# Bias tables of an encoder kernel: 32 copies of each bias row made by the matmul, a 128-partition store, and a skewed read back in four pieces

## The chip, the cores and the metric

The kernel runs on one core of one Trainium2 chip. The metric is the device time of one execution in microseconds (us). Before the change three runs took 1973.15, 1976.38 and 1978.78 us; the median is 1976.38 us.

## What is computed

The reference is a two-layer encoder over a sample of 512 tokens and a prompt of 256 tokens, width 1024. Layer 0 mixes tokens with a gated linear recurrence (4 heads of 128, 64-token chunks, both directions) and with dilated band attention: three groups of four heads of 64, with windows and dilations (128, 1), (512, 4) and (2048, 16). Layer 1 mixes with a gated 31-tap depthwise convolution. Each layer ends with a squared-ReLU MLP of width 4096 and layer norms.

The change touches one piece of the attention, its additive bias:

```python
rel = c - QB - a                                   # key position minus query position
valid = (np.abs(rel) <= half)[None] & (key_idx >= 0) & (key_idx < L)
bias = jnp.transpose(bias_table[t5_buckets(rel * r)], (2, 0, 1))
s = jnp.einsum('brhnqd,brhnkd->brhnqk', qb, kb) * (dh ** -0.5) + bias[:, None]
s = jnp.where(valid, s, NEG_INF)
```

The bias of a head depends on the relative position alone: 383 values per head (`RELW`), looked up in a table of 32 buckets by 12 heads, plus the band limit (a very large negative number outside it).

## The kernel before, in words

Tokens of both inputs stand side by side (768 columns: 512 sample, 256 prompt). Every large product is made of three products of a high and a low half (`split`, lines 132 to 135: ScalarE copies a tile to the high half, `wh` or `x0h`, VectorE or GpSimd subtracts to get the low half, `wl` or `x0l`). Weights come in units of 128x1024 floats: `advance` (lines 137 to 147) loads one through SyncE's queue into one of 3 `raw` buffers and splits it. `gemm_fm` (line 167) turns one unit into 128 output features for all tokens: 24 matmuls of 512 columns and 24 of 256, in two of the three PSUM buffers with the tag `g`. `gemm_tm` (line 181) makes token-major products.

Layer 0 (`ab_layer`) goes: load and split the input (`load_x`), make the bias tables (`bias_tables`), then for each attention group `attn_gemm` (four units of queries and keys, drained by ScalarE at line 454 and VectorE at line 456, then six token tiles of values, drained at lines 471 and 473) and `attention` (jobs of score, softmax, transpose and value product, six jobs in group 0 and three in each of the others). Groups 1 and 2 write their values to DRAM (`dv<-mv`, line 479) and read them back permuted (line 485). Then follow `cross_group`, the recurrence, and the rest.

`bias_tables` needs, for each group, a tile in which partition p holds, for each of the four heads, the bias row shifted by p. It multiplies the bucket table by a one-hot matrix (line 408, 4 partitions out), adds the band limit on VectorE into a row tile (line 412, or a copy at line 414), stores the row 128 times to DRAM from these 4 partitions with GpSimd's queue (line 416, `bt<-qq`), and reads it back with a stride of 382 floats per partition, which makes the skew (line 421, `r<-bt`). For groups 1 and 2 VectorE adds block masks to it (lines 426 and 428). The row tile has the tag `qq`, and there is one buffer of it: the next group's row waits until the store of this one has landed. At the end a selection matrix is loaded into the one `e` buffer and copied by GpSimd to `selr` (lines 431 to 433), which takes the same `qq` buffer. The `e` and `at` buffers are also those in which every second attention job keeps its scores (line 522); the `mv` buffers (two) hold one-hot rows, block masks and later the values of groups 1 and 2.

The order of the instructions on each engine is fixed when the kernel is built, by a scheduler with its own model of what each instruction costs; each engine then works through its own queue in that order and waits where an operand or a buffer is not ready. GpSimd's DMA issues stand in GpSimd's queue, and a DMA that must wait for another holds what is behind it there.

Of the kernel before, what the change touches and what calls it, by code (L numbers as in the profile page):

```python
# [11 lines left out]
F32 = mybir.dt.float32  # L12
# [3 lines left out]
ALU = mybir.AluOpType  # L16
# [4 lines left out]
P = 128  # L21
# [4 lines left out]
T = TS + TP  # L26
# [36 lines left out]
NEG = -1e30  # L63
# [3 lines left out]
BUCKETS = 32  # L67
MAXDIST = 1024
TAPS = 31
HALO = TAPS // 2  # L70
RELW = 383
UPAD = TS + TP + 3 * HALO
UOUT = TS + TP + HALO
SEG = ((0, TS), (TS, TP))
AB = {"g": 8, "e": 1, "at": 1, "qq": 1, "mv": 2, "oa": 4, "ob": 6}
# [3 lines left out]
def _buckets(rel):  # L79
    half = BUCKETS // 2  # L80
    exact = half // 2
    n = np.abs(rel)
    large = exact + (np.log(np.maximum(n, 1) / exact) / np.log(MAXDIST / exact) * (half - exact)).astype(np.int32)
    large = np.minimum(large, half - 1)
    return np.where(rel > 0, half, 0) + np.where(n < exact, n, large)


def _fm(w):
    n = w.shape[1] // P
    return w.reshape(KD, P, n, P).transpose(2, 1, 0, 3).reshape(n, P, D)  # L90


def _bm(w, nf):
    k = w.shape[0] // P
    q = D // nf
    n = w.shape[1] // nf
    return w.reshape(k // q, q, P, n, nf).transpose(0, 3, 2, 1, 4).reshape(k // q, n, P, D)


class Kernel:  # L100
# [292 lines left out]

    def bias_tables(self):
        nc, i = self.nc, self.i
        rb = self.sb(self.abc, [BUCKETS, 12], "rb")
        nc.gpsimd.dma_start(rb, i["rel_bias"])
        oh = self.t("e")[0:BUCKETS].rearrange("p (a b) -> p a b", a=2)
        oh2 = self.t("mv")[0:BUCKETS, 0:384]
        nc.gpsimd.dma_start(oh[:, :, 0:RELW], i["onehot"][:, 0:2, :])  # L400
        nc.gpsimd.dma_start(oh2[:, 0:RELW], i["onehot"][:, 2, :])
        bm = self.t("at")[0:4].rearrange("p (a b) -> p a b", a=2)
        nc.gpsimd.dma_start(bm[:, :, 0:RELW], i["band"].partition_broadcast(4))
        self.bt = []
        for g in range(3):
            p = self.ps("s")
            src = oh[:, g, 0:RELW] if g < 2 else oh2[:, 0:RELW]
            mm = nc.tensor.matmul(p[0:4, 0:RELW], rb[:, 4 * g : 4 * g + 4], src, start=True, stop=True)
            self.after(mm, self.mark, SYNC)
            row = self.sb(self.ap, [P, 2, T], "qq", bufs=AB["qq"])[0:4, 0, 0:384]  # L410
            if g < 2:
                nc.vector.tensor_tensor(row[:, 0:RELW], p[0:4, 0:RELW], bm[:, g, 0:RELW], ALU.add)
            else:
                nc.vector.tensor_copy(row[:, 0:RELW], p[0:4, 0:RELW])
            dt = self.dram.tile([4, P, RELW], F32, tag=f"bt{g}", name=f"bt{g}")
            nc.gpsimd.dma_start(dt, row[:, None, 0:RELW].to_broadcast([4, P, RELW]))
            t = self.sb(self.rp, [P, D], "r")
            w = 256 if g == 0 else 128
            shift = RELW // 2 - (64 if g == 0 else 0)
            src = bass.AP(tensor=dt.tensor, offset=dt.offset + shift, ap=[[RELW - 1, P], [P * RELW, 4], [1, w]])  # L420
            nc.gpsimd.dma_start(t[:, 0 : 4 * w].rearrange("p (h c) -> p h c", h=4), src)
            if g:
                bk = self.t("mv")[:, 0 : 2 * P].rearrange("p (a b) -> p a b", a=2)
                nc.gpsimd.dma_start(bk, i["block"][:, 2 * (g - 1) : 2 * g, :])
                v = t.rearrange("p (s h c) -> p s h c", s=2, h=4)
                nc.vector.tensor_tensor(v[:, 1], v[:, 0], bk[:, 1][:, None, :].to_broadcast([P, 4, P]), ALU.add)
                if g == 2:
                    nc.vector.tensor_tensor(v[:, 0], v[:, 0], bk[:, 0][:, None, :].to_broadcast([P, 4, P]), ALU.add)
            self.bt.append(t)
        sel = self.t("e")[0:12]  # L430
        nc.gpsimd.dma_start(sel, i["sel"].rearrange("r j p -> r (j p)"))
        self.selr = self.sb(self.ap, [P, 2, T], "qq", F32R, AB["qq"])[0:12, 0, :].rearrange("r (j p) -> r j p", j=6)
        nc.gpsimd.tensor_copy(self.selr.rearrange("r j p -> r (j p)"), sel)
# [681 lines left out]
def layout(x_prompt, x_sample, rel_bias, hgrn_lb, w_in_ab, hgrn_norm, w_out_ab, w_in_c, b_in_c, dw_c, dw_b_c, cnorm_g,  # L1115
           cnorm_b, w_out_c, b_out_c, ln_mix_g, ln_mix_b, mlp_w1, mlp_w2, ln_ffn_g, ln_ffn_b):
    a = {k: np.asarray(v, dtype=np.float32) for k, v in locals().items()}
    x = np.concatenate([a["x_sample"][0], a["x_prompt"][0]], 0)
    w = a["w_in_ab"][0]
    hw = 5 * AW  # L1120
    bcols = []
    for g in range(3):
        for part in range(2):
            s = hw + part * BW + g * 256
            bcols.append(w[:, s : s + 256])
    acols = []
    for h in range(4):
        for part in (0, 2, 3, 4):
            s = part * AW + h * P
            acols.append(w[:, s : s + P])  # L1130
    woab = a["w_out_ab"][0]
    woab = np.concatenate([woab[AW:], woab[:AW]], 0)
    rel = np.arange(RELW) - RELW // 2
    onehot = np.zeros((BUCKETS, 3, RELW), np.float32)
    band = np.zeros((2, RELW), np.float32)
    for g, (win, r) in enumerate(GROUPS):
        b = _buckets(rel * r)
        onehot[b, g, np.arange(RELW)] = 1.0
        if g < 2:
            band[g] = np.where(np.abs(rel) <= win // (2 * r), 0.0, NEG)  # L1140
    idx = np.arange(P)
    block = np.zeros((P, 4, P), np.float32)
    for n, ln in enumerate((128, 64, 32, 16)):
        block[:, n, :] = np.where(idx[:, None] // ln == idx[None, :] // ln, 0.0, NEG)
    lmask = np.zeros((P, 5, P), np.float32)
    for n, s in enumerate((1, 2, 4, 8)):
        lmask[:, n, :] = (idx[:, None] // (2 * s) == idx[None, :] // (2 * s)) & (idx[:, None] // s != idx[None, :] // s)
    lmask[:, 4, :] = idx[:, None] // 16 != idx[None, :] // 16
    sel = np.zeros((12, 6, P), np.float32)
    for j in range(6):  # L1150
        sel[2 * j, j, 0:64] = 1.0
        sel[2 * j + 1, j, 64:128] = 1.0
    vec = np.concatenate([
        a["dw_c"][0].T, a["b_in_c"][0].reshape(2, D).T, a["dw_b_c"][0][:, None], a["cnorm_g"][0][:, None],
        a["cnorm_b"][0][:, None], np.zeros((D, 1), np.float32)], 1)
    out = {
        "x": x,
        "xT": x.T.reshape(KD, P, T),
        "w_b": _fm(np.concatenate(bcols, 1)),
        "w_vb": _bm(w[:, hw + 2 * BW :], 256),  # L1160
        "w_va": _bm(w[:, AW : 2 * AW], 512),
        "w_a": _fm(np.concatenate(acols, 1)),
        "w_oab": _bm(woab, 512),
        "w1": np.stack([_fm(a["mlp_w1"][l]) for l in range(DEPTH)]),
        "w2": np.stack([_bm(a["mlp_w2"][l], 512) for l in range(DEPTH)]),
        "w_c": _fm(a["w_in_c"][0]),
        "w_oc": _bm(a["w_out_c"][0], 512),
        "rel_bias": a["rel_bias"],
        "lbT": a["hgrn_lb"].reshape(2, 3, 4, P).transpose(3, 0, 1, 2),
        "gnT": a["hgrn_norm"][0].reshape(4, P).T,  # L1170
        "vecC": vec.reshape(KD, P, 37).transpose(1, 0, 2),
        "bo": a["b_out_c"][0],
        "ln0": np.stack([a["ln_mix_g"][0], a["ln_mix_b"][0]]),
        "ln1": np.stack([a["ln_ffn_g"][0], a["ln_ffn_b"][0]]),
        "ln2": np.stack([a["ln_mix_g"][1], a["ln_mix_b"][1]]),
        "ln3": np.stack([a["ln_ffn_g"][1], a["ln_ffn_b"][1]]),
        "ident": np.eye(P, dtype=np.float32),
        "onehot": onehot,
        "band": band,
        "block": block,  # L1180
        "lmask": lmask,
        "sel": sel,
    }
    return {k: np.ascontiguousarray(v) for k, v in out.items()}
# [13 lines left out]
```

## Time and profile before

| | |
|---|---|
| median of three runs | 1976.38 us (1973.15 to 1978.78) |
| span of the profiled execution, first to last instruction | 1977.0 us |
| PE busy (TensorE matmul) | 1855.2 us, 94% |
| VectorE busy | 1149.4 us, 58% |
| ScalarE busy | 737.5 us, 37% |
| GpSimd busy | 595.4 us, 30% |
| PE busy from 0 to 300 us | 231.79 us |
| PE busy from 300 us to the end | 1623.44 us of 1677 us |

The page gives the span of the profiled execution and no other time of it; the span lies within the spread of the three runs. Busy time of an engine says how long its instructions ran, not what they waited for; the granted clock of TensorE is given as a share of full speed (1.00 is 2.4 GHz, 0.50 is 1.2 GHz).

### The profile page before, as it was taken

To read this page: it belongs to the slowest core of one execution; us is meant where nothing else is said; L and a number is where in the kernel's file an instruction comes from. 1 tells how busy PE (TensorE), PEld (TensorE's weight loads), DVE (VectorE), ACT (ScalarE), POOL (GpSimd) and SP (SyncE) were. 2 spreads that over 40 slices of the span, in tenths; PEclk is the share of its full clock that TensorE was granted. 3 is DMA by queue.
4 is the path that set the end of the run, shared out by engine and by line. 5 is a ranking of instruction groups with operands and counts; after the bars stand their busy time and mean duration, and the time that the engine had idled before them with its cause. 6 is when DMAs were issued, how large, how long until landed. Compare 5 with 4: busy or idle time off the path is not lost.

```text
span 1977.0 us, 26150 instructions
## 1 busy us (share of the span) xinstructions
PE 1855.2 (94%) x10516; PEld 1578.5 (80%) x10516; DVE 1149.4 (58%) x1816; ACT 737.5 (37%) x1200; POOL 595.4 (30%) x355
## 2 busy tenths in 40 slices
PE   5964999999999999999999999889999999999998
PEld 4854787888878888888878989768888789888886
DVE  3221643666676634333469999888995554433336
ACT  3210631233421433333354435644433545423322
POOL 1000100544431000000047668646544468000002
PEclk9986998999999999999999999989999999999999
DMA  5323122111021423333235445433433356412211
GB/s 169 93 49 76 28 78 81 44 44 43 33 97 36 139 96 98 105 96 96 86 102 160 134 141 178 134 110 117 131 96 96 95 160 190 141 54 64 75 43 64
DMA packets 58108, 191.36 MB, mean 97 GB/s; under 512 B 8396, under 2 KB 11532, under 8 KB 57988
## 3 DMA queue, kind: packets, MB, share of 16 engines
q1 hardware_dynamic: 52196, 177.23, 28.9%
q0 software_dynamic: 4928, 9.32, 2.4%
q10 hardware_dynamic: 864, 3.15, 0.5%
q8 instruction: 82, 1.34, 0.3%
q14 instruction: 38, 0.31, 0.1%
HBM read 182.50 MB, written 7.15 MB: 96 GB/s over the span
## 4 chain that ended last, share of the span: by engine, by line
PE 80%; DVE 10%; DMA 4%; issue 3%; ACT 2%; POOL 1%; SPq 0%; DVEq 0%; ACTq 0%; POOLq 0%
PE g L167 41%; PE s L181 24%; PE g L181 7%; PE s L976 3%; DMA raw<-w_b 2%; DMA dv<-mv 2%; DVE qq L731 1%; DVE at L774 1%; DVE x0l L135 1%; ACT wh L134 1%; DVE g L732 1%; DVE w L1078 1%; DVE r L241 1%; PE s L580 1%; PE s L527 0%
## 5 line engine op out<-in xcount | busy, mean ns | idle before, releaser
L134 ACT ACTIVATE wh<-raw 128x1024 fp32r<-128x1024 f32 x320 | 339.0, 1060 | 753.5 <-PE g L167 306.6
L135 POOL TENSOR_TENSOR wl<-raw,wh 128x1024 fp32r<-128x1024 f32 x168 | 411.2, 2457 | 224.2 <-ACT wh L134 223.2
L181 PE MATMUL s<-wh,t 128*128 128x512 f32 x1280 | 398.0, 389 | 1.5 <-DVE r L241 1.5
L167 PE MATMUL g<-x0h,wh 128*128 128x512 f32 x864 | 341.0, 395 | 31.7 <-DVE mv L471 22.3
L135 DVE TENSOR_TENSOR wl<-raw,wh 128x1024 fp32r<-128x1024 f32 x152 | 186.8, 1229 | 268.5 <-ACT wh L134 268.4
L167 PE MATMUL g<-x0l,wh 128*128 128x512 f32 x864 | 339.9, 394 | 0.0
L167 PE MATMUL g<-x0h,wl 128*128 128x512 f32 x864 | 338.7, 392 | 0.0
L181 PEld LDWEIGHTS s<-wh,t 128*128 128x128 f32 x1280 | 240.3, 188 | 52.3 <-DVE r L241 1.9
L167 PE MATMUL g<-x1h,wh 128*128 128x256 f32 x864 | 247.5, 287 | 15.6 <-ACT g L454 15.5
L1017 DVE SCALAR_TENSOR_TENSOR c<-t,vec,c 128x509 f32<-128x509 f32 (+26 forms) x464 | 250.0, 604 | 1.1
L167 PE MATMUL g<-x1h,wl 128*128 128x256 f32 x864 | 247.9, 287 | 1.7 <-DVE wl L135 1.7
L181 PE MATMUL s<-wl,t 128*128 128x512 f32 x640 | 249.1, 389 | 0.0
L167 PE MATMUL g<-x1l,wh 128*128 128x256 f32 x864 | 247.9, 287 | 0.3 <-DVE x1l L135 0.2
L220 POOL TENSOR_TENSOR r<-r,lb 128x512 f32<-128x512 f32 x20 | 29.2, 1482 | 623.2 <-DVE r L219 623.2
L167 PEld LDWEIGHTS g<-x0h,wh 128*128 128x128 f32 x864 | 163.2, 189 | 66.7 <-DVE mv L471 22.5
L241 DVE TENSOR_TENSOR r<-r,s 128x512 f32<-128x512 f32 x164 | 112.1, 684 | 153.9 <-PE s L181 151.3
L167 PEld LDWEIGHTS g<-x0h,wl 128*128 128x128 f32 x864 | 163.3, 189 | 34.5 <-DVE wl L135 0.8
L167 PEld LDWEIGHTS g<-x0l,wh 128*128 128x128 f32 x864 | 163.4, 189 | 33.8 <-DVE x0l L135 1.4
L167 PEld LDWEIGHTS g<-x1h,wh 128*128 128x128 f32 x864 | 167.9, 195 | 18.9 <-ACT g L454 16.0
L939 DVE TENSOR_TENSOR t<-t,t 128x512 fp32r<-128x512 f32 (+1 forms) x112 | 94.4, 843 | 137.2 <-ACT t L938 137.0
L167 PEld LDWEIGHTS g<-x1l,wh 128*128 128x128 f32 x864 | 168.4, 195 | 3.1 <-DVE x1l L135 0.7
L167 PEld LDWEIGHTS g<-x1h,wl 128*128 128x128 f32 x864 | 168.4, 195 | 2.2 <-DVE wl L135 2.0
(335 smaller groups left out, 2525.3 us busy)
## 6 DMA issues: line engine op xcount, KB each, us to landing
raw<-w SPq DMA_DIRECT2D x224, 512.0 KB
raw<-w_c SPq DMA_DIRECT2D x32, 512.0 KB
raw<-w_a SPq DMA_DIRECT2D x16, 512.0 KB
raw<-w_oc SPq DMA_DIRECT2D x16, 512.0 KB
raw<-w_b SPq DMA_DIRECT2D x12, 512.0 KB
raw<-w_oab SPq DMA_DIRECT2D x10, 512.0 KB
raw<-w_vb SPq DMA_DIRECT2D x6, 512.0 KB
r<-x ACTq DMA_DIRECT2D x6, 512.0 KB
```

The lines of the kernel that those rows point to most:

```text
L134: nc.scalar.activation(hi, src, AF.Copy)
L135: return (eng or nc.vector).tensor_tensor(lo, src, hi.bitcast(F32), ALU.subtract)
L167: mm = nc.tensor.matmul(p[:, 0:n], w, x[:, k, :], start=k == 0 and j == 0, stop=k == KD - 1 and j == 2)
L181: nc.tensor.matmul(out, a, w, start=k == 0 and j == 0, stop=k == n - 1 and j == 2)
L220: eng.tensor_tensor(half[q], half[q], b[q], ALU.add)
L241: self.nc.vector.tensor_tensor(dst, dst, p, ALU.add)
L580: nc.tensor.matmul(po[64 * e : 64 * e + 64, c0 : c0 + rows], vv, pts[e][:, b * P : b * P + rows], start=n == 0, stop=n == len(kts) - 1)
L731: eng.tensor_tensor(qv, qv, tv[:, :, kh : kh + 1].to_broadcast([P, n, s]), ALU.mult)
L732: eng.tensor_tensor(kv, kv, tv[:, :, qh : qh + 1].to_broadcast([P, n, s]), ALU.mult)
L939: nc.vector.tensor_tensor(lo, rl, hi.bitcast(F32), ALU.subtract)
L976: self.nc.tensor.matmul(p, x, y, start=u == 0 and k == 0 and j == 0, stop=u == 3 and k == 1 and j == 2)
L1017: nc.vector.scalar_tensor_tensor(dst, src, tap, dst, ALU.mult, ALU.add)
```

## The change

The bucket table gets a 33rd row of ones and the one-hot matrix a 33rd row with the band limit, so that the product holds the band limit already. GpSimd copies each head's column of the table 32 times side by side (`rep`), so that the product comes out on 128 partitions: 32 equal rows for each of four heads. One tile of the tag `qq` holds the rows of all three groups side by side. The store to DRAM is now 128 rows of 383 floats, one row from each partition, a quarter of the bytes of before. The read back has four DMAs for each table, one for each 32 partitions; each reads 32 skewed rows of four heads. The block masks are added by GpSimd instead of VectorE. The load of the band limit on four partitions goes away.

```diff
-        bm = self.t("at")[0:4].rearrange("p (a b) -> p a b", a=2)
-        nc.gpsimd.dma_start(bm[:, :, 0:RELW], i["band"].partition_broadcast(4))
+        rep = self.t("at")[0:nr, 0 : 12 * REP].rearrange("p (a b) -> p a b", b=REP)
+        nc.gpsimd.memset(rep[BUCKETS:nr], 1.0)
+        nc.gpsimd.tensor_copy(rep[0:BUCKETS], rb.unsqueeze(2).to_broadcast([BUCKETS, 12, REP]))
+        rows = self.sb(self.ap, [P, 2, T], "qq", bufs=AB["qq"]).rearrange("p a b -> p (a b)")
...
-            mm = nc.tensor.matmul(p[0:4, 0:RELW], rb[:, 4 * g : 4 * g + 4], src, start=True, stop=True)
+            mm = nc.tensor.matmul(p[:, 0:RELW], rep[:, 4 * g : 4 * g + 4, :], src, start=True, stop=True)
             self.after(mm, self.mark, SYNC)
-            row = self.sb(self.ap, [P, 2, T], "qq", bufs=AB["qq"])[0:4, 0, 0:384]
-            if g < 2:
-                nc.vector.tensor_tensor(row[:, 0:RELW], p[0:4, 0:RELW], bm[:, g, 0:RELW], ALU.add)
-            else:
-                nc.vector.tensor_copy(row[:, 0:RELW], p[0:4, 0:RELW])
-            dt = self.dram.tile([4, P, RELW], F32, tag=f"bt{g}", name=f"bt{g}")
-            nc.gpsimd.dma_start(dt, row[:, None, 0:RELW].to_broadcast([4, P, RELW]))
+            row = rows[:, g * 384 : g * 384 + RELW]
+            nc.vector.tensor_copy(row, p[:, 0:RELW])
+            dt = self.dram.tile([P, RELW], F32, tag=f"bt{g}", name=f"bt{g}")
+            nc.gpsimd.dma_start(dt, row)
...
-            src = bass.AP(tensor=dt.tensor, offset=dt.offset + shift, ap=[[RELW - 1, P], [P * RELW, 4], [1, w]])
-            nc.gpsimd.dma_start(t[:, 0 : 4 * w].rearrange("p (h c) -> p h c", h=4), src)
+            for a in range(P // REP):
+                src = bass.AP(tensor=dt.tensor, offset=dt.offset + shift - REP * a,
+                              ap=[[RELW - 1, REP], [REP * RELW, 4], [1, w]])
+                dst = t[REP * a : REP * (a + 1), 0 : 4 * w].rearrange("p (h c) -> p h c", h=4)
+                nc.gpsimd.dma_start(dst, src)
             if g:
...
-                nc.vector.tensor_tensor(v[:, 1], v[:, 0], bk[:, 1][:, None, :].to_broadcast([P, 4, P]), ALU.add)
+                nc.gpsimd.tensor_tensor(v[:, 1], v[:, 0], bk[:, 1][:, None, :].to_broadcast([P, 4, P]), ALU.add)
                 if g == 2:
-                    nc.vector.tensor_tensor(v[:, 0], v[:, 0], bk[:, 0][:, None, :].to_broadcast([P, 4, P]), ALU.add)
+                    nc.gpsimd.tensor_tensor(v[:, 0], v[:, 0], bk[:, 0][:, None, :].to_broadcast([P, 4, P]), ALU.add)
```

## Rows read from the trace of the kernel before

**Rows 1.** Waits of PE, 0 to 300 us: total, times, longest.

```profile
PE g L167 <- DVE mv L471: 22.3, 1, 22.3
PE g L181 <- ACT mv L473: 21.5, 1, 21.5
PE g L167 <- ACT g L454: 15.9, 2, 15.5
```

**Rows 2.** Timeline of PE: start us, duration us, instruction, idle before it.

```profile
21.19 0.40 PE L167 MATMUL g<-x0h,wh 128*128 128x512 f32 x1
...
29.53 0.40 PE L167 MATMUL g<-x0h,wh 128*128 128x512 f32 x1
...
50.69 0.58 PE L167 MATMUL g<-x1h,wh 128*128 128x256 f32 x1 [15.54 <-ACT g L454]
```

**Rows 3.** Chain that ended last, 0 to 300 us: start us, duration us, what.

```profile
64.11 17.28 PE g L181 x144
...
152.15 32.20 DMA dv<-mv
```

**Rows 4.** Timeline of ScalarE (ACT), 21 to 56 us.

```profile
42.12 1.06 ACT L134 ACTIVATE wh<-raw 128x1024 fp32r<-128x1024 f32 x1 [20.34 <-DMA raw<-w_vb]
49.10 1.06 ACT L134 ACTIVATE wh<-raw 128x1024 fp32r<-128x1024 f32 x1 [5.92 <-DMA raw<-w_vb]
50.06 0.58 ACT L454 ACTIVATE g<-g 128x512 f32<-128x512 f32 x1
```

**Rows 5.** Timeline of SyncE's DMA issues (SPq), 0 to 260 us.

```profile
18.73 6.19 SPq L142 DMA_DIRECT2D raw<-w_vb  x2
```

**Rows 6.** Timeline of GpSimd (POOL), 0 to 260 us.

```profile
16.89 1.17 POOL L416 DMA_DIRECT2D bt<-qq  x1
...
53.68 0.78 POOL L421 DMA_DIRECT2D r<-bt  x1 [35.07 <-DMA bt<-qq]
111.52 1.13 POOL L416 DMA_DIRECT2D bt<-qq  x1 [57.06 <-DVE qq L412]
...
185.50 0.81 POOL L433 CAST qq<-e 12x768 fp32r<-12x768 f32 x1
```

**Rows 7.** Timeline of VectorE (DVE), 14 to 260 us.

```profile
15.60 0.54 DVE L412 TENSOR_TENSOR qq<-c,at 4x383 f32<-4x383 f32 x1
...
110.68 0.54 DVE L412 TENSOR_TENSOR qq<-s,at 4x383 f32<-4x383 f32 x1
...
147.03 0.55 DVE L414 COPY qq<-c 4x383 f32<-4x383 f32 x1 [21.64 <-DMA bt<-qq]
150.68 0.69 DVE L426 TENSOR_TENSOR r<-r,mv 128x512 f32<-128x512 f32 x1 [3.11 <-DMA r<-bt]
```

**Rows 8.** Windows: length, PE busy (matmuls), granted clock, DMA share, GB/s.

```profile
140.00:150.00 10.00, 0.00 (x0) 0.50 0.25 47
150.00:160.00 10.00, 8.10 (x52) 0.69 0.36 51
160.00:170.00 10.00, 2.67 (x23) 0.82 0.25 27
...
180.00:190.00 10.00, 5.05 (x12) 0.50 0.34 61
190.00:200.00 10.00, 10.00 (x57) 0.98 0.63 198
...
210.00:220.00 10.00, 9.06 (x74) 0.66 0.02 2
```

**Rows 9.** DMA issues, 0 to 300 us: KB of each, median us to landing.

```profile
bt<-qq POOLq DMA_DIRECT2D x3, 766.0 KB, 36.1
...
r<-bt POOLq DMA_DIRECT2D x1, 512.0 KB, 4.3
...
scr<-mx POOLq DMA_DIRECT2D x16, 4.0 KB, 2.4
```

**Rows 10.** One line (L220), whole run: duration ns min/median/max.

```profile
L220 POOL TENSOR_TENSOR r<-r,pt x4: 1287/1479/1677, 621.0 to 628.1; 128x512 f32<-128x512 f32 x4
```

More of the change, by code (lines that the diff above doesn't have):

```diff
@@ L71 @@
 RELW = 383
+REP = 32
 UPAD = TS + TP + 3 * HALO
@@ L395, in bias_tables @@
         nc, i = self.nc, self.i
+        nr = BUCKETS + 1
         rb = self.sb(self.abc, [BUCKETS, 12], "rb")
         nc.gpsimd.dma_start(rb, i["rel_bias"])
-        oh = self.t("e")[0:BUCKETS].rearrange("p (a b) -> p a b", a=2)
-        oh2 = self.t("mv")[0:BUCKETS, 0:384]
+        oh = self.t("e")[0:nr].rearrange("p (a b) -> p a b", a=2)
+        oh2 = self.t("mv")[0:nr, 0:384]
         nc.gpsimd.dma_start(oh[:, :, 0:RELW], i["onehot"][:, 0:2, :])
         nc.gpsimd.dma_start(oh2[:, 0:RELW], i["onehot"][:, 2, :])
-        bm = self.t("at")[0:4].rearrange("p (a b) -> p a b", a=2)
-        nc.gpsimd.dma_start(bm[:, :, 0:RELW], i["band"].partition_broadcast(4))
+        rep = self.t("at")[0:nr, 0 : 12 * REP].rearrange("p (a b) -> p a b", b=REP)
+        nc.gpsimd.memset(rep[BUCKETS:nr], 1.0)
+        nc.gpsimd.tensor_copy(rep[0:BUCKETS], rb.unsqueeze(2).to_broadcast([BUCKETS, 12, REP]))
+        rows = self.sb(self.ap, [P, 2, T], "qq", bufs=AB["qq"]).rearrange("p a b -> p (a b)")
         self.bt = []
@@ L1133, in layout @@
     rel = np.arange(RELW) - RELW // 2
-    onehot = np.zeros((BUCKETS, 3, RELW), np.float32)
-    band = np.zeros((2, RELW), np.float32)
+    onehot = np.zeros((BUCKETS + 1, 3, RELW), np.float32)
     for g, (win, r) in enumerate(GROUPS):
@@ L1139, in layout @@
         if g < 2:
-            band[g] = np.where(np.abs(rel) <= win // (2 * r), 0.0, NEG)
+            onehot[BUCKETS, g] = np.where(np.abs(rel) <= win // (2 * r), 0.0, NEG)
     idx = np.arange(P)
@@ L1178, in layout @@
         "onehot": onehot,
-        "band": band,
         "block": block,
```

## The prediction, made blind

> **What bounds the kernel now.** I read the busy shares first: PE runs 94% of the span, 1623 of the 1677 us after 300 us, but only 232 of the first 300. So what can be won lies in the first 300 us, and the list of what PE waited for there comes next. Three single waits hold nearly all of it: 15.5 us until ScalarE drained a PSUM buffer at L454, 21.5 us until ScalarE drained a value tile at L473, 22.3 us until VectorE drained one at L471 [rows 1, 2]. None is the fault of the engine named; the timelines of the queues say what each drain stood behind.
>
> Wait A (PE idle from 35.15 to 50.69): the drain at L454 runs at 50.06, right behind the splits of the two `w_vb` weight units, and ScalarE had waited for these loads until 42.12 and 49.10 [rows 4]. The two were issued between 18.73 and 24.9 [rows 5], so a 512 KB load took over 20 us. What was in flight beside them is the first table store, issued at 16.89 and landed at 53.68 [rows 6].
>
> Wait B (21.5 us, ending at 152): GpSimd issues the second table store at 111.52 [rows 6]. VectorE's copy of the third row at 147.03 had to wait for it to land, 21.64 us, because there is one row buffer; the block add at 150.68 waited again for the read back; the drains of group 1's values stand behind these [rows 7].
>
> Wait C (22.3 us, ending at 185): the store of group 1's values, issued at 152.15, takes 32.20 us [rows 3] and holds a value buffer. Again a table store runs beside it: the third, issued as soon as the second has landed.
>
> So all three are one thing, the table store: 766 KB, 36.1 us to landing, three times [rows 9]. From 140 to 150, when PE did nothing and nothing else was being loaded, the 16 DMA engines were busy 0.25 of the time [rows 8]: four engines' worth of work. The Trainium skill, page "DMA: Bandwidth & Descriptors", section "Why a DMA increments its semaphore by 16 and not by 1", says that a copy is spread over the largest number of engines, at most 16, that divides the slowest dimension of both its patterns; for an array that begins with 4 that is four engines, and the trace's 0.25 agrees. By that rule the new store, with 128 in front, runs on all 16.
>
> **The store and the read back after the change.** Before, the store was 512 rows of 1532 bytes; on four engines that is 128 rows each in 36.1 us, 0.28 us a row. Now it is 128 rows. On 16 engines that is 8 rows, 2.3 us; were it still four, 32 rows, 9.0 us. The 4 KB store of softmax statistics, also one piece from each of 128 partitions, takes 2.4 us to land [rows 9], which I add as what a store costs with almost nothing in it: 4.7 us by the one, 11.4 us by the other. I take 4.7, because the shape is that of the 2.4 us row; 11.4 stays as the other end.
>
> The twelve reads replace three. A whole 512 KB read landed in 4.3 us, and its issue took GpSimd 0.78 us [rows 6, 9]; a piece of a quarter is bounded by these from above, and by the 2.4 us of the small transfer from below. GpSimd's queue then looks like this: the three rows are copied at 15.60 and the two slots behind it (0.54 us each, [rows 7]), done by 17.2; three store issues of at most 1.17 us, 20.7; landed by 25.4; twelve read issues of at most 0.78 us, 34.8; landed by 39.1; the three block adds, 1.48 us each on GpSimd [rows 10], by about 44 us at the latest. With 11.4 us stores everything moves to about 50. If nothing overlapped at all, the stores and group 0's four reads would be through at 17.2 + 3 x 4.7 + 4 x (0.78 + 4.3) = 51.6, and the last read at 92.
>
> The table of group 0 is needed by the first attention job. One unit of queries or keys takes PE 29.53 - 21.19 = 8.34 us [rows 2], the value product 17.28 us [rows 3]; from 21.19 three units and the values end at 63.5. Group 1's table is needed 33.4 + 17.3 us later, at 114. So all of the table work lies beside matmuls with 13 us or more to spare, and costs nothing; without that cover each late microsecond costs one.
>
> A rule of the skill speaks against the change: the same page, section "Anatomy of one DMA — SWDGE (gpsimd) path", gives each DMA a fixed cost of about 2 us whatever its size. The row of 2.4 us for 4 KB agrees. There are nine DMAs more on the tables, so 18 us more if each cost stood on the path, and the sum below would end near 1930; by the slack just worked out it doesn't stand there.
>
> **The sum, against the span of 1977.0 us.**
> - Wait A and its slow restart: without it the value product of group 0 would end at 63.5; it ends at 64.11 + 17.28 = 81.4 [rows 3]. Minus 17.9 us.
> - Waits B and C: minus 21.5 and 22.3 us [rows 1].
> - Slow restarts behind B and C: 75 matmuls of L181 took 8.10 + 2.67 us at granted clocks of 0.69 and 0.82 [rows 8]; at 17.28/144 = 0.120 us each they would take 9.0. The 69 of L167 from 180 to 200 took 15.05, where 8.34/48 = 0.174 us each makes 12.0. Minus 1.8 and 3.0 us.
> - Group 0's attention was late, too: its odd jobs need the `e` buffer, which the selection matrix held until GpSimd copied it at 185.50 [rows 6], as that copy needs the row buffer. So they ran when few matmuls of group 1 were left to cover them; from 210 to 220 PE was idle for 0.94 us and at clock 0.66 [rows 8]. At full clock its 9.06 us would be 6.0, so between 0 and 4 us are to be had; I take 2.
> - Added: three row copies on VectorE where there was one at that point, among the input splits, 2 x 0.54 = 1.1 us at most, none at least, as the next unit starts only at 21.19. I take 1.1.
> - Added: the matmuls keep their 383 columns; that the results are on 128 partitions instead of 4 adds no columns. `rep` is one small GpSimd fill and one copy of 384 elements, some 0.8 us by the copy of 768 elements [rows 6], while the matmuls wait for the input splits anyway. The load of the band limit goes, unseen.
> - What is late next: the values of group 1. If the second half still has to wait for the store of the first, it waits for a store without the table's beside it: between 0 and the 4.3 us of a 512 KB transfer. I take 3.
>
> Together: 17.9 + 43.8 + 4.8 + 2.0 - 1.1 - 3.0 = 64.4 us less, 1912.6 from the span. The span is 0.6 us above the median of the runs, so 1912. The ends of the likeliest case: all of the slow attention won and nothing added gives 1906, one more wait of some ten microseconds 1922; another order written by the scheduler after 300 us may add or take a few.
>
> **The rivals.**
> 1. Wait A stays in part. The stores and reads of all three tables are now packed between 17 and 39 us, where two `w_vb` loads are in flight, and ScalarE's drain still stands behind their splits. PE needs that drain at 35.15, so the second load must land by about 33, within 8 us of its issue at the latest. For it: from 190 to 200 the engines moved 198 GB/s at a share of 0.63 [rows 8]; three loads (1.6 MB) and the tables (0.6 MB stored, 1.0 MB read) are 3.2 MB in some 15 us, 213 GB/s, which isn't far from that. Against it: the store no longer sits on four engines that every load needs. Price 1 to 17.9 us, the time up to 1930.
> 2. Wait C comes back from GpSimd. The block adds now free the `mv` buffers that group 1's values need, and they stand in GpSimd's queue with the statistics stores, which wait for attention. If the scheduler puts an add behind such a store, PE waits at the values as before: 22.3 + 3.0 us, 1937. Against it: before the first job GpSimd has nothing else to do.
> 3. Slower: the tables come late. The order will put group 0's attention into the queues of PE, VectorE and ScalarE from 63.5 us on, where it stood behind the waits before. If the stores keep their 36.1 us and follow one another, and each piece costs its issue and landing with group 0's pieces last, the tables are there at 17.2 + 3 x 36.1 + 12 x 5.1 = 187; PE stands from 63.5, 123 us, less the 64 won: 2035. This decides against the change from a table later than 128 us. Against it: a quarter of the bytes, and 128 partitions to take them from.
> 4. Nothing won, because the scheduler leaves the row copies and reads where they were (the second row copy at 110.68). For it: that order came from its own costs. Against it: the copy stood there because the row buffer was taken; now all three rows have their own columns. 1976.
>
> **How the numbers follow.** The forecast has 0.74; wait A in part 0.12; wait C again 0.07; late tables 0.04; nothing won 0.01; and 0.02 for a gain above the bounds, by an order that is better elsewhere. The range 1898 to 1938 takes in the bounds of the unknown terms and the first two rivals. A change of under 0.3%, 6 us, is about what the three runs before can't tell from none (they spread over 5.6 us). Faster by more than that: 0.74 + 0.12 + 0.07 + 0.02 = 0.95; the same 0.01; slower 0.04.
>
> **What would show it.** In the trace after: three table stores landing in under 12 us each, all issued before 30 us; no wait of PE above 6 us in the first 200 us; the value product of group 0 ending at 63 to 66 us and that of group 2 some 66 us earlier; a granted clock of 1.00 from 20 us to 180. A drain at L454 that runs after 36 us shows rival 1, a drain at L471 or L473 that waits for GpSimd rival 2, PE waiting for a bias add at L532 or L537 rival 3. The prediction is wrong if PE's idle time in the first 300 us doesn't fall from 68 us (300 - 231.79) to under 20, or if it falls and the idle time after 300 us grows from 54 us by more than ten.

## The result, and the profile after

The changed kernel takes 1909.12 us (median of four runs, 1906.43 to 1911.25) against 1977.58 us for the kernel before on the same chip: a ratio of 0.9665, with a 95% interval of 0.9649 to 0.9682, 68 us less. The forecast was 1912. The profiled execution took 1907.15 us and spans 1905.1 us, 71.9 less than the span before. The ratio is the result; 71.9 compares two single executions.

PE's waits in the first 300 us, total, times and longest:

```profile
PE g L168 <- ACT wh L135: 7.5, 1, 7.5
PE s L565 <- ACT sb L558: 1.0, 1, 1.0
PE g L168 <- DVE x0l L136: 0.2, 1, 0.2
PE c L565 <- DVE pt L571: 0.2, 1, 0.2
```

The three waits of [rows 1] are gone (lines are a few numbers further down: L454 is now L458, L471 and L473 are L475 and L477). What is left is the first wait of all, for the first weights, which the kernel before had too (7.1 us); by its 7.5 us the sign "no wait of PE above 6 us in the first 200 us", as the prediction words it, was missed. PE is busy 290.91 of the first 300 us, where it was 231.79; the columns are length, PE busy, clock, DMA share, GB/s:

```profile
0.00:300.00 300.00, 290.91 (x1832) 0.98 0.31 94
300.00:1905.10 1605.10, 1553.47 (x8686) 0.99 0.33 101
```

Its idle time falls from 68 to 9 us in the first 300 us, and from 54 to 52 us behind them.

The windows that answer to [rows 8]; the columns are PE, weight loads, VectorE, ScalarE and GpSimd, each with its instructions, then the granted clock, the DMA share and GB/s:

```profile
20.00:30.00 10.00, 10.00 (x62) 8.95 (x61) 4.29 (x8) 2.55 (x5) 6.06 (x11) 1.00 1.00 233
30.00:40.00 10.00, 10.00 (x57) 8.75 (x56) 4.87 (x5) 3.94 (x5) 5.08 (x5) 1.00 0.79 215
...
60.00:70.00 10.00, 9.01 (x61) 7.00 (x59) 6.54 (x13) 5.20 (x13) 0.37 (x1) 1.00 0.19 54
...
130.00:140.00 10.00, 10.00 (x101) 9.65 (x99) 3.46 (x7) 2.50 (x3) 0.00 (x0) 1.00 0.18 48
140.00:150.00 10.00, 9.93 (x83) 7.09 (x81) 7.77 (x27) 7.92 (x36) 2.18 (x4) 1.00 0.48 153
...
180.00:190.00 10.00, 10.00 (x84) 9.92 (x83) 3.36 (x4) 1.44 (x2) 0.00 (x0) 1.00 0.18 60
```

The clock is 1.00 in these and in all other such windows up to 230 us, where it was 0.50 to 0.82 around the waits. The DMA engines are busy all of the time from 20 to 30 us, and PE does not wait. The chain of waits shows where group 2's value product begins and how long it takes:

```profile
16.42 29.81 PE g L168 x175
46.24 15.85 PE g L182 x132
...
183.41 17.28 PE g L182 x144
```

Group 0's value product begins at 46.24; 144 matmuls at its pace end at 63.5, the forecast's figure, where [rows 3] gave 81.4. Group 2's begins at 183.41; in the kernel before it began at 253.20:

```profile
253.20 17.28 PE g L181 x144
```

The DMA issues that answer to [rows 9], KB of each and median us to landing, and GpSimd's timeline that answers to [rows 6]:

```profile
bt<-qq POOLq DMA_DIRECT2D x3, 191.5 KB, 4.4
r<-bt POOLq DMA_DIRECT2D x4, 128.0 KB, 6.8
r<-bt POOLq DMA_DIRECT2D x8, 64.0 KB, 7.8
```

```profile
16.59 0.58 POOL L417 DMA_DIRECT2D bt<-qq  x1
...
17.81 1.08 POOL L417 DMA_DIRECT2D bt<-qq  x2
20.24 4.47 POOL L425 DMA_DIRECT2D r<-bt  x8 [1.35 <-DMA bt<-qq]
...
33.93 1.28 POOL L430 TENSOR_TENSOR r<-r,mv 128x512 f32<-128x512 f32 x1 [4.14 <-DMA r<-bt]
35.17 0.57 POOL L425 DMA_DIRECT2D r<-bt  x1
...
39.26 2.15 POOL L432 TENSOR_TENSOR r<-r,mv 128x512 f32<-128x512 f32 x1
```

A store lands in 4.4 us instead of 36.1. All three are issued by 19 us, and the last block add ends at 41.4. ScalarE's drain, which answers to [rows 4], runs at 31.20, 4 us ahead of the 35.15 at which PE ran dry before:

```profile
25.12 1.06 ACT L135 ACTIVATE wh<-raw 128x1024 fp32r<-128x1024 f32 x1 [3.48 <-DMA raw<-w_vb]
30.24 1.06 ACT L135 ACTIVATE wh<-raw 128x1024 fp32r<-128x1024 f32 x1 [4.06 <-DMA raw<-w_vb]
31.20 0.58 ACT L458 ACTIVATE g<-g 128x512 f32<-128x512 f32 x1
```

### The profile page after: what moved, and what is told of

Same layout as the page of the kernel before. It is cut to its first block, busy times and chain, and to the rows that moved or that the text cites. A ratio compares the mean times of both kernels' runs of the same rounds, so it can differ in the third digit from the quotient of the medians.

```text
span 1905.1 us, 26155 instructions
## 1 busy us (share of the span) xinstructions
PE 1844.4 (97%) x10516; PEld 1569.5 (82%) x10516; DVE 1146.5 (60%) x1813; ACT 738.2 (39%) x1200; POOL 603.3 (32%) x368
## 4 chain that ended last, share of the span: by engine, by line
PE 85%; DVE 11%; ACT 1%; issue 1%; POOL 1%; DMA 1%; SPq 0%; DVEq 0%; ACTq 0%; POOLq 0%
PE g L168 44%; PE s L182 25%; PE g L182 7%; PE s L980 3%; DVE qq L735 1%; DVE at L778 1%; DVE w L1082 1%; DVE x0l L136 1%; DVE g L736 1%; DVE r L242 1%; DVE x1l L136 1%; ACT wh L135 0%; DVE g L737 0%; DVE w L1083 0%; PE s L531 0%
```

## The experiments

Theory at the outset: a store costs by the rows that each DMA engine has to move; the old store held four engines with 128 rows each, and all that stood behind or beside it waited. Rivals: the single row buffer, the bytes, and the table's lateness as such. Every kernel is timed against the kernel before on its own chip. The runs are called one_tile, sixteen, fewer_bytes, four_stores, rows_124, row_in_turn, adds_on_vector, late_table and reads_twice, in the order in which they come.

### One row tile, everything else as before

```diff
+        rows = self.sb(self.ap, [P, 2, T], "qq", bufs=AB["qq"]).rearrange("p a b -> p (a b)")
...
-            row = self.sb(self.ap, [P, 2, T], "qq", bufs=AB["qq"])[0:4, 0, 0:384]
+            row = rows[0:4, g * 384 : (g + 1) * 384]
```

> The kernel before with one edit: the three bias rows stand side by side in one row tile, so that no row copy waits for a store. The stores are left as they were, 766 KB from 4 partitions. Theory (what costs is how long a store holds four DMA engines and what stands behind it): each store still takes about 36 us to land, so wait A (the drain at L454 behind the w_vb loads) stays, 16 us or more, and more if two stores in flight share the same four engines; waits B and C go, since no copy and no value store stands beside a table store any more: 1977 - 44 - 5 = about 1928 us, 1940 if A grows. Rival (the single row buffer is the whole cost): all three waits go, 1909 us.

1957.14 us, ratio 0.9909 (0.9894 to 0.9924). A miss for both. PE's longest waits, the stores, and one window (length, PE busy, clock, DMA share, GB/s) while two stores are in flight:

```profile
PE g L167 <- ACT g L455: 44.5, 1, 44.5
...
PE g L181 <- ACT mv L474: 2.5, 1, 2.5
```

```profile
bt<-qq POOLq DMA_DIRECT2D x3, 766.0 KB, 65.3
```

```profile
50.00:60.00 10.00, 0.00 (x0) 0.50 0.47 33
```

Waits B and C go, as the theory said, and wait A grows from 15.5 to 44.5 us: the row buffer had kept two stores apart. But two stores took 65 us at a share of 0.47, twice one store's share. They do keep eight engines busy, and are no faster for it: 2 x 784 thousand bytes (766 KB of 1024 bytes each) in 65 us are 24 GB/s, one store alone in 36.1 us made 22. That speaks against a price per row on an engine.

### The same bytes from 16 partitions

```diff
...
+        nc.gpsimd.tensor_copy(rep, rb.unsqueeze(2).to_broadcast([BUCKETS, 12, 4]))
...
-            mm = nc.tensor.matmul(p[0:4, 0:RELW], rb[:, 4 * g : 4 * g + 4], src, start=True, stop=True)
+            mm = nc.tensor.matmul(p[0:16, 0:RELW], rep[:, 4 * g : 4 * g + 4, :], src, start=True, stop=True)
...
-            nc.gpsimd.dma_start(dt, row[:, None, 0:RELW].to_broadcast([4, P, RELW]))
+            nc.gpsimd.dma_start(dt, row[:, None, 0:RELW].to_broadcast([16, 32, RELW]))
```

> The kernel before with one edit: the matmul makes four copies of each head's row, so that a store starts from 16 partitions, each repeated 32 times: the same 766 KB in the same 512 rows of 1532 bytes, the same single row buffer, one read for each table, the adds on VectorE. Theory (rows per DMA engine): 32 rows an engine at 0.28 us and 2.4 us for a small store make 11.4 us to landing; the DMA share while it runs is near 1.0 instead of 0.25; waits A, B and C go: 1910 to 1918 us. Rival (the bytes cost, wherever they come from): a store still takes 36 us or close to it, the waits stay, 1960 us or more.

1910.37 us, ratio 0.9671 (0.9657 to 0.9686); no wait of PE above 1 us behind the first weights. Its stores:

```profile
bt<-qq POOLq DMA_DIRECT2D x3, 766.0 KB, 9.9
```

So the bytes by themselves are not the cost: all 766 KB are stored three times, through one row buffer, with the adds on VectorE, and the whole gain is there.

The scheduler's order changes with the store, too. The second store is issued at 40.27 here (39.37 in the next kernel), where the kernel before has 111.52 [rows 6]:

```profile
40.27 0.64 POOL L418 DMA_DIRECT2D bt<-qq  x1 [11.51 <-DVE qq L414]
```

The first store, beside which wait A arose, stands at 17 to 18 us in all three. How much of waits B and C went by the shorter store and how much by its earlier place, these two runs do not tell.

### A quarter of the bytes from 4 partitions

```diff
-            nc.gpsimd.dma_start(dt, row[:, None, 0:RELW].to_broadcast([4, P, RELW]))
+            nc.gpsimd.dma_start(dt, row[:, None, 0:RELW].to_broadcast([4, 32, RELW]))
```

(with the four reads of the changed kernel and a DRAM tile of 32 copies; both are left out here.)

> The kernel before with one edit: the row is stored 32 times instead of 128 (192 KB) and the table read back in four pieces; the store still starts from 4 partitions, with one row buffer and the adds on VectorE. Theory (rows per DMA engine): again 32 rows an engine, 11.4 us to landing at a share near 0.25, the same as with sixteen partitions and four times the bytes; 1910 to 1918 us. Rival (four partitions are slow in themselves, or a store has a long fixed part): landing stays above 20 us and wait A stays in part, 1925 us or more.

1906.40 us, ratio 0.9651 (0.9635 to 0.9667). Its stores land as late as those from 16 partitions with four times the bytes, as expected:

```profile
bt<-qq POOLq DMA_DIRECT2D x3, 191.5 KB, 10.3
```

Both runs fit rows per engine. They fit as well a price on the partitions read from, since four partitions and four engines, 16 and 16, go together in them. The next run takes them apart.

### Four stores from the same 4 partitions

```diff
-            nc.gpsimd.dma_start(dt, row[:, None, 0:RELW].to_broadcast([4, P, RELW]))
+            for c in range(4):
+                nc.gpsimd.dma_start(dt[:, 32 * c : 32 * (c + 1), :], row[:, None, 0:RELW].to_broadcast([4, 32, RELW]))
```

> The kernel before with each table store split into four of 32 copies, issued one behind the other: the same 766 KB from the same 4 partitions, on four sets of four engines instead of one if each DMA takes the next set. In the kernel with one row tile two stores in flight took 65 us instead of 36 at a DMA share near 0.5, which speaks against my price of 0.28 us a row on an engine. Theory A (a row costs an engine 0.28 us): the four are done in about 11.4 us at a share near 1.0, waits A, B and C shrink to under 10 us in all, 1910 to 1925 us. Theory B (4 partitions give out some 22 GB/s, whatever the number of engines that read from them): still 36 us, at a share near 1.0, all engines held; wait A as before or longer, 1970 us or more.

1972.01 us, ratio 0.9986 (0.9964 to 1.0008). PE's waits, the stores, and one window (length, GpSimd busy, clock, DMA share, GB/s):

```profile
PE g L181 <- ACT mv L474: 20.8, 1, 20.8
PE g L167 <- ACT g L455: 19.4, 1, 19.4
PE g L167 <- DVE mv L472: 17.8, 1, 17.8
```

```profile
bt<-qq POOLq DMA_DIRECT2D x12, 191.5 KB, 31.1
```

```profile
30.00:40.00 10.00, 0.00 (x0) 0.90 0.96 26
```

All three waits are back. The stores stand where they did in the kernel before (the second at 115 us). The engines are busy 0.96 of the time and move 26 GB/s. In the kernel with 16 partitions the same share goes with 298 GB/s, while weights are loaded (same columns):

```profile
25.00:30.00 5.00, 0.78 (x1) 1.00 0.96 298
```

The four quarter stores together, 32 rows on each of 16 engines if each takes the next four, take 31.1 us where the store from 16 partitions takes 9.9. Theory A falls; B stands: in these runs the partitions that a store comes from set its pace, and a busy share near 1 does not say that the engines move much.

### 124 partitions

```diff
-            nc.gpsimd.dma_start(dt, row)
+            nc.gpsimd.dma_start(dt[0:124], row[0:124])
+            nc.gpsimd.dma_start(dt[124:P], row[124:P])
```

> The changed kernel with each table store split into one from 124 partitions and one from the last 4. By the Trainium skill, page "DMA: Bandwidth & Descriptors", section "Why a DMA increments its semaphore by 16 and not by 1", 124 is spread over 4 engines, or over 16 by the exception that the section names. Theory A (a row costs an engine 0.28 us): on 4 engines 31 rows each, the store lands after 11 us. Theory B (the partitions that it comes from set the pace): it lands after 4 to 6 us on 4 engines as on 16. The time of the whole kernel is the same by both, 1904 to 1915 us.

1908.83 us in one run. The store from 124 partitions lands in 3.8 us, no later than the one from 128:

```profile
bt<-qq POOLq DMA_DIRECT2D x3, 185.5 KB, 3.8
```

That agrees with theory B. It proves less than it was meant to, as the trace does not tell on how many engines the store ran: the share near it (0.64 to 0.81) holds the weight loads too.

### Parts taken back

The row buffer in turn, in the changed kernel:

```diff
-        rows = self.sb(self.ap, [P, 2, T], "qq", bufs=AB["qq"]).rearrange("p a b -> p (a b)")
...
-            row = rows[:, g * 384 : g * 384 + RELW]
+            row = self.sb(self.ap, [P, 2, T], "qq", bufs=AB["qq"])[:, 0, 0:RELW]
```

> The changed kernel with one part taken back: each group's row gets the one row buffer in turn, so that a row copy waits for the store of the row before. Theory: a store lands in 4.4 us, so VectorE waits under 5 us twice in the first 35 us, the last table comes some 9 us later than in the changed kernel, and nothing that PE needs comes later: within 0.3% of the changed kernel, 1904 to 1915 us. Rival (the row buffer was a cost of its own): wait of VectorE's weight splits behind the copies reaches PE, 5 to 20 us, 1914 to 1930 us.

1907.40 us, ratio 0.9661 (0.9647 to 0.9675), with PE's waits as in the changed kernel. The adds on VectorE (`nc.gpsimd.tensor_tensor` back to `nc.vector.tensor_tensor` in three lines):

> The changed kernel with one part taken back: the three block adds are on VectorE again. PE's, ScalarE's and SyncE's orders are those of the changed kernel. Theory: adds on either engine are covered, since the first group that needs them begins at 138 us; VectorE waits at them a few us for the reads, before 45 us; the same time within 0.3%, 1904 to 1915 us. Rival (the adds on VectorE hold weight splits back, as in the kernel before): PE waits for a low half behind them, 2 to 8 us.

1906.33 us, ratio 0.9651 (0.9637 to 0.9666), PE's waits again the same. Neither part wins or loses anything that these runs can tell.

### A late table, without DMA work

```diff
+            for _ in range(80 if g == 0 else 0):
+                nc.gpsimd.memset(t, 0.0)
             for a in range(P // REP):
```

> The changed kernel with GpSimd kept busy by 80 fills of the table tile of group 0 (128x1024 each, an estimate of 1.05 us each by the fill of 384 elements that took 0.41 us) ahead of its four reads, with no DMA added: the table of group 0 comes near 110 us instead of 30, and the scheduler, which knows of the fills, puts group 0's attention behind the matmuls of group 1. Theory (the waits came from what stood behind a DMA, not from the table being late as such): PE keeps matmuls to do, and only the uncovered attention costs, under 6 us: 1909 to 1916 us. Rival (a late table is itself the loss, one microsecond for each after 64): 40 us or more, 1950 us.

1907.29 us, ratio 0.9671 (0.9637 to 0.9705). The first bias add, on VectorE, and the window of PE ahead of it:

```profile
109.02 0.69 DVE L538 TENSOR_TENSOR sb<-s,r 128x512 f32<-128x512 f32 x1 [4.07 <-DMA r<-bt]
```

```profile
100.00:110.00 10.00, 10.00 (x85) 1.00 0.47 147
```

Group 0's attention starts at 109 us instead of 65, and PE loses nothing by it that the time shows: a table that is late, and known to be late when the order is written, costs nothing here. In the kernel before it started at 115:

```profile
114.95 0.68 DVE L532 TENSOR_TENSOR sb<-s,r 128x512 f32<-128x512 f32 x1
```

There the read of group 0's table had been issued at 53.68, as soon as its store had landed, and the second row copy stood in VectorE's queue until 110.68 [rows 6, 7]. So that late start was in the order itself. What the scheduler reckons for such a store, and what it leaves out, no run shows.

### The reads twice

```diff
+            t2 = self.sb(self.rp, [P, D], "r")
...
                 nc.gpsimd.dma_start(dst, src)
+                more = t2[REP * a : REP * (a + 1), 0 : 4 * w].rearrange("p (h c) -> p h c", h=4)
+                nc.gpsimd.dma_start(more, src)
```

> The changed kernel with each of the twelve reads issued a second time into a spare tile, 1.0 MB more between 20 and 50 us, when the DMA engines are already busy 0.8 to 1.0 of the time. In the changed kernel the drain behind the w_vb loads ran at 31.2 and PE needs it by about 35. Theory (rival 1 of the prediction was real, and the change passes it by 4 us): with 4 to 8 us more of DMA work ahead of or beside the two loads the drain comes near or past 35 and PE waits there again, 0 to 5 us: 1909 to 1914 us, seen in the waits of PE rather than in the time. Other theory (the loads have their own way and the reads don't hold them): the drain stays within 1 us of 31.2.

1907.60 us, ratio 0.9651 (0.9633 to 0.9670). The drain:

```profile
30.61 0.58 ACT L461 ACTIVATE g<-g 128x512 f32<-128x512 f32 x1
```

It comes no later than in the changed kernel, so the other theory holds as far as the run reaches: only about half of the added megabyte was issued before the second `w_vb` load had landed at 29.6 us, and that half did not hold the loads back. What a whole megabyte ahead of them would do is not shown.

## Why the prediction was right

**What bounds.** That the three waits are one thing, the table store, was right. [rows 4 to 7] named it; one_tile shows it from one side (A grows with the store's time), four_stores from the other (all three return though each DMA has a quarter of the bytes). What ties a load to the store is in the trace of the kernel before, while the second `w_vb` load was still on its way (length, GpSimd busy, clock, DMA share, GB/s):

```profile
40.00:45.00 5.00, 0.00 (x0) 0.51 0.25 44
```

Three quarters of the engines' time is free, and the load is not done until 49.1 [rows 4]: its rest seems to lie on the engines that the store holds. The same share stands at 160 to 170 us [rows 8], when the value store of wait C was under way. The window of 140 to 150 that the prediction read was not empty of other transfers: group 1's table was read from 147.28 on.

**The store's price, the step that failed.** The prediction read the share of 0.25 [rows 8] as four engines, which agrees with the count in the Trainium skill, page "DMA: Bandwidth & Descriptors", section "Why a DMA increments its semaphore by 16 and not by 1", and went on to charge a row to an engine at 0.28 us. The count may stand; the charge does not. Four_stores has 32 rows on an engine and takes 31.1 us, not 11.4. The rates that the runs give, bytes over time to landing: from 4 partitions 22 GB/s (one store), 24 (two at once), 25 (four at once, 784 thousand bytes in 31.1 us). With the 2.4 us of a tiny store taken off each, an estimate, these are 23, 25 and 27; 196 thousand bytes from 4 partitions in 10.3 us make 25 GB/s, and 784 thousand from 16 partitions in 9.9 us make 105. The Trainium skill, page "SBUF — State Buffer", section "Door 1: The DMA port swizzle (why `[64,N]` ≈ `[32,N]`)", says that bandwidth goes by how many of 16 ports the partitions reach, and gives partitions 0 to 3 one port with 27.6 GB/s, partitions 0 to 15 four with 104. These runs come near both, 23 to 27 and 105. The section that the prediction went by speaks of engines alone. Whether a port sets the pace or each partition its own, no run here separates. The 4.7 us for the new store came near the 4.4 measured by luck: 2.3 of them are eight rows at a price that four_stores refutes. The sum did not hang on it: the stores of fewer_bytes land after 10.3 us, and the whole gain is there.

**The reads.** The bound from above failed: 6.8 and 7.8 us to landing, not at most 4.3. The row of 4.3 us was one read with no other table read beside it; of the twelve, eight are issued in 4.5 us, beside weight loads, at a share of 1.00. The step bore it: the last add ended at 41.4 where "44 us at the latest" was said.

**The sum.** Wait A: 17.9 us forecast, and the value product ends at 63.5 as forecast. Up to the start of group 2's value product the gain is 253.20 - 183.41 = 69.8 us, 64.4 forecast. Of that, 17.9, 43.8 and 4.8 were charged to the waits and restarts; the remaining 3.3 would lie within the 0 to 4 of group 0's attention, where I took 2. The two costs that were added did not come: PE waits for no value drain any more (3 taken, 0 measured), and the next unit starts at 21.05, not later than the 21.19 of [rows 2] (1.1 taken for the copies, 0 measured). The 2.1 us more from there to the end are no gain that I can name: four executions of the changed kernel span 1904.7 to 1909.4 us. The split over waits B, C and the attention is worked out, not measured apart, as the new order moved all three.

**The rivals.** Rival 1 (wait A in part): 4 us from coming true by the clock; in reads_twice half a megabyte more of table reads beside the loads did not bring it nearer. Rival 2 (adds on GpSimd behind the statistics stores): the adds ran by 41 us, the first such store at 69. Rival 3 (late tables) fell with its condition: the stores land after 4.4 us, not 36.1. late_table does not test it, since there the order was written for the late table; it shows that such lateness, up to 109 us, is free. Rival 4: the row copies start at 15.56, 16.96 and 17.43 us.

## What to carry to other kernels

A store from four partitions ran at 22 to 27 GB/s here, however its rows were cut and however many engines it held, and weight loads and value stores beside one of 766 KB took 20 us and more. Look for it where a load of ordinary size takes 20 us, not where the DMA itself stands. Spread the source over partitions first (16 were enough here), or cut its bytes; either alone gave the whole gain here, 3.3 and 3.5%. A busy share of the DMA engines is not throughput: read the GB/s beside it.

## What the runs showed that was not expected

Two stores in flight from the same four partitions keep twice as many engines busy and land after some 65 us each, half as fast as one alone. Four keep 0.96 of the engines busy at 26 GB/s, and ScalarE waits 28.3 us for a 512 KB weight load beside them. A table that comes some 80 us later costs nothing that the time shows when the order was written for it.
